# Second down-projection as seven products of quarters, with the quarter sums on GpSimd

## The chip, the cores and the metric

The kernel runs on one core of a Trainium2 chip. The time is device microseconds of one execution: 2637.14 us is the median of three runs before the change (2635.62 to 2639.12).

A core has engines with a queue of their own each: TensorE (PE in the profile; PEld is its loading of weights), VectorE (DVE), ScalarE (ACT), GpSimd (POOL) and SyncE (SP), which issues all DMAs here. Matrix products land in PSUM, eight banks of 128x512 numbers; all other tiles lie in SBUF.

## The reference: what is computed

One layer over 1024 latent tokens (and 256 context tokens) of width 1024: a half-step SwiGLU, two attention mixers with a merge, and a second half-step SwiGLU. The change is in the last of these:

```python
def _swiglu(h, w1, w3, w2):
    return (jax.nn.silu(h @ w1) * (h @ w3)) @ w2
...
        x = _residual(x, _swiglu(_modnorm(x, g[4], m[6], m[7]), ffn2_w1[l], ffn2_w3[l], ffn2_w2[l]),
                      g[5], m[8], HALF_STEP)
```

`D_FF` is 2816, so the last product is [1024 tokens x 2816] times [2816 x 1024]. `_residual` normalises each token's row of the product, scales it by a gate, and adds it to x.

## The kernel before, in words

*Precision.* Every float32 operand of a large product is split in two: `split` (L202) lets ACT cast it to the high part and DVE subtract that from the operand for the low part. `mm3` (L158) then issues three matmuls: high with high, high with low, low with high. A matmul has a 128x128 stationary and a 128x512 moving operand and writes one bank.

*Pools.* SBUF tiles come from pools: `U` and `V` (24 and 16 tiles of 128x1024), `T2` (20 tiles of 128x512). PSUM banks have the tags s, m and v (3, 3 and 2 buffers).

*Order.* The kernel's author writes the order out: a `Plan` (L163) has main steps, most of them groups of matmuls, and `spread` puts side work (loads, splits, sums) behind the main steps with given numbers. Engines keep this order, and each waits for what it needs by semaphores. `store` (L134) issues its DMA some main steps later (2 if no number is given), so that SP is not held.

*Second up-projection* (`up_units`, L700). `Unit` (L494) makes 256 rows of h @ w1 or h @ w3 from quarters, by seven products of 12 matmuls in place of eight; the sums that this takes are made by DVE from SBUF (`Unit.sum`) or while it empties banks (`p6`, `p5`, `p7`, `p3`, `p4`). A w1 unit and a w3 unit make a pair, eleven pairs in all; `emit1` applies SiLU, `emit3` multiplies and stores the gated quarter, 128 rows of D_FF by 512 tokens, into a DRAM tensor. The first 14 units are led: their first two products run ahead as one step each (`plan_leads`), and five are left. The other 8 run whole, seven products. A product of 12 matmuls is one main step.

*Second down-projection* (`Down`, L729). It walks over the 22 chunks of 128 rows of D_FF in ten groups, nine of two chunks and one of four. In each group every one of the 8 token tiles and 2 output halves gets a bank, 3 matmuls per chunk; ACT copies the first group's banks into the output tiles (V), DVE adds those of the others. Gated rows and weights come back from DRAM as 128x1024 tiles and are split, three steps ahead and more. Beside it runs `ada_steps((8,))`: the row of the last modulation, 16 DVE operations of 128x512. `gate_rows` turns it into a row for all tokens (8 small transposes).

*End* (L2066 to L2118). With the last group each finished token tile is squared by ACT, POOL makes the reciprocal root (two operations of 128x1), DVE multiplies by the gate, scales and adds x, and SP stores. The last tile goes in halves.

Of the kernel before, what the change touches and what calls it, by code (L numbers as in the profile page):

```python
# [10 lines left out]
BF16 = mybir.dt.bfloat16  # L11
# [32 lines left out]
def hybrid_block(ctx: ExitStack, tc: tile.TileContext, a: dict, out: bass.AP):  # L44
# [25 lines left out]
    def V(dt=F32):  # L70
        return U(dt, "v")
# [16 lines left out]
    def PB(tag):  # L88
        return ps.tile([P, 512], F32, tag=tag, name=nm("b" + tag), bufs=PBUFS[tag])
# [22 lines left out]
    class Engine:  # L112


        def __init__(self, e):
            self.e = e
# [132 lines left out]
    class Ada:  # L249
# [20 lines left out]

        def turn(self):
            rows = self.rows
            pt = PB("v").rearrange("p (t g c) -> p t g c", t=4, c=32)
# [41 lines left out]
    class AdaSum(Ada):  # L315


        def __init__(self, m):
            self.m = m
            self.acc = [[T2() for _ in range(2)] for _ in range(2 if m < 5 else 1)]  # L320

        def load(self, k, h):
# [10 lines left out]
                    vec.scalar_tensor_tensor(t[h], r, sc[:, k, v:v + 1], t[h], op0=ALU.mult, op1=ALU.add)  # L333

        def add_up(self):
            self.bank = PB("v")
# [9 lines left out]
    def ada_steps(ms):  # L346

        s = []
        cur = {}

        def step(m, k, h):
            if m not in cur:
                cur[m] = AdaSum(m)
# [28 lines left out]
    def gate_rows(col, key="u"):  # L382
        row = U(key=key)
        for h in range(2):
            pb = PB("s")
            for k in range(4):
                turn_(pb[:, k * P:(k + 1) * P], col[:, 4 * h + k:4 * h + k + 1].to_broadcast([P, P]), ident)
            act.copy(row[:, h * 512:(h + 1) * 512], pb)
        return row
# [307 lines left out]
                plan.spread([f], at[t] + x, at[t] + x + 1)  # L697


    def up_units(h, w1, w3, gd):  # L700

        units = []

        def pair_(p):
            s = {}

            def emit1(i, ci, x, bank):
                s[i, ci] = T2() if bank else x
# [12 lines left out]
        return units  # L721
# [7 lines left out]
    class Down:  # L729
# [26 lines left out]
        def tile(self, t, es=range(2)):  # L756
            ys, fs = self.ys, self.fs
            g = self.g if t < 8 else self.c
            c = slice((t % 8) * P, (t % 8 + 1) * P)
            if fs[0] == 0 and 0 in es:  # L760
                ys[t] = V()
            for e in es:
                o = slice(e * 512, (e + 1) * 512)
                pd = PD()
                for x, f in enumerate(fs):
                    mm3(pd, [y[:, c] for y in g[f]], self.w[f][e], x == 0, x == len(fs) - 1)
                if fs[0] == 0:
                    act.copy(ys[t][:, o], pd)
                else:
                    vec.tensor_tensor(ys[t][:, o], ys[t][:, o], pd, op=ALU.add)  # L770

    def groups(sizes):
# [1222 lines left out]
    gd2 = DR([NF, P, NLAT])  # L1995
    units2 = up_units(h3, a["f2w1"], a["f2w3"], gd2)
    plan = Plan()
    for f in set0[6:] + wsets[1].loads():
# [51 lines left out]
    plan.spread([normal_banks], e - 1, e)  # L2050
    plan_rest(plan, units2)

    gs = groups((2,) * 9 + (4,))
    ys2 = {}
    downs2 = [Down(a["f2w2"], gd2, ys2, fs) for fs in gs]
    o = len(plan.main)
    plan.spread([lambda: downs2[0].loads(0, "u")], o - 9, o - 8)
    plan.spread(downs2[0].steps(key="u"), o - 7, o)

    def last_col():  # L2060
        cols["g8"] = gate_col(8, 5, 0, 0.5)

    def last_gates():
        cols["g8"] = gate_rows(cols["g8"], "v")

    def done2(t, x):  # L2066
        y = ys2[t]
        if x == 0:
            xr, r, z = V(), rstd(y, D), V()
# [10 lines left out]
    def done_half(e):  # L2080

        y, o = ys2[7], slice(e * 512, e * 512 + 512)
        if e == 0:
            end.update(x=V(), z=V(), ss=ST(2), junk=T2(BF16, 1024))
            ld(end["x"], x2s[7 * P:8 * P, :])
        z, ss = end["z"], end["ss"]
        act.activation(end["junk"][:, o], y[:, o], AF.Square, scale=D ** -0.5, accum_out=ss[:, e:e + 1])
        if e == 0:
            pool.tensor_scalar(ss[:, 0:1], ss[:, 0:1], EPS, None, op0=ALU.add)
            vec.tensor_tensor(z[:, o], y[:, o], cols["g8"][:, o], op=ALU.mult)  # L2090
            return
        r = ST()
        act.activation(ss[:, 1:2], ss[:, 1:2], AF.Identity, bias=ss[:, 0:1])
        pool.tensor_tensor(r, ss[:, 1:2], mhalf[:, 0:1], op=ALU.pow)
        vec.tensor_tensor(z[:, o], y[:, o], cols["g8"][:, o], op=ALU.mult)
        for h in range(2):
            o = slice(h * 512, h * 512 + 512)
            vec.scalar_tensor_tensor(z[:, o], z[:, o], r, end["x"][:, o], op0=ALU.mult, op1=ALU.add)
            store(out[7 * P:8 * P, o], z[:, o], 0)

    d2_at = len(plan.main)
    for i, d in enumerate(downs2):
        o = len(plan.main)
        if i + 1 < len(downs2):
            plan.step(*[lambda d=d, t=t: d.tile(t) for t in range(8)])
        else:
            plan.step(*[lambda d=d, t=t: d.tile(t) for t in range(7)], *[lambda d=d, e=e: d.tile(7, (e,)) for e in range(2)])
        if i + 1 < len(downs2):
            n = downs2[i + 1]
            plan.spread([lambda n=n: n.loads(n.fs[0])], o - 1, o)  # L2110
            plan.spread(n.steps(), o + 1, o + 8)
        else:
            plan.spread([last_col], o - 3, o - 2)
            plan.spread([last_gates], o - 1, o)
            for t in range(7):
                plan.spread([lambda t=t: done2(t, 0)], o + t, o + t + 1)
                plan.spread([lambda t=t: done2(t, 1)], o + t + 1, o + t + 2)
            plan.spread([lambda e=e: done_half(e) for e in range(2)], o + 7, o + 9)  # L2118
# [80 lines left out]
```

## Time and profile before

| what | value |
|---|---|
| median of the runs | 2637.14 us |
| profiled execution, span of its instructions | 2632.2 us |
| PE busy | 2602.1 us, 13728 matmuls |
| DVE busy | 1854.2 us |
| ACT busy | 1151.8 us |
| POOL busy | 220.3 us, 368 instructions |
| second up-projection, after the leading products | 2041.2 to 2383.7 us |
| second down-projection | 2383.7 to 2625.2 us |
| DMA in all | 414.14 MB, mean 157 GB/s |

The profiled execution's own time is known by its span alone, from its first instruction to its last; the runs' times hold a few microseconds around it. Start times count from the span's start. A row of a timeline has the start, the length, the engine, the line, the operation, the tiles written and read (buffer numbers left out) and, in brackets, the idle time before it and what ended that. A row of groups has the number of instructions, their busy time, the mean length of one in ns, and the idle time before them with its releasers. Tiles are named by pool: xu, xv and t for U, V and T2, bs, bm and bv for the banks, st for small statistics, d for DRAM. The line of most instructions is that of a helper (L120 for DVE, ACT and POOL, L153 for matmuls, L132 for DMAs), so the tiles tell more.

### The profile page before, as it was taken

The numbers are of one execution on the slowest core, as the hardware profiler recorded it, in microseconds if no ns is written. First come the engines' busy times: TensorE is split into PE (matmuls) and PEld (weight loads), VectorE is DVE, ScalarE is ACT, GpSimd is POOL, SyncE is SP. The second block draws the span as 40 slices with busy tenths as digits, with TensorE's granted clock in tenths as the row PEclk, the third lists the DMA queues.
The fourth block names the chain that finished last, engine by engine and source line by source line (L and its number), as shares of the span: only waits on it lengthen the run. The fifth ranks groups of instructions, "written<-read, shape, count | busy, mean of one in ns | idle before, by whom it ended". The sixth has DMA issues, their size and how long they took to land.

```text
span 2632.2 us, 37730 instructions
## 1 busy us (share of the span) xinstructions
PE 2602.1 (99%) x13728; PEld 2215.3 (84%) x13728; DVE 1854.2 (70%) x3478; ACT 1151.8 (44%) x2193; POOL 220.3 (8%) x368
## 2 busy tenths in 40 slices
PE   8999999999999999999999999999999999999998
PEld 6888888888888788889889999987888888888887
DVE  4778876588776676864569988877436777565876
ACT  6622223522223753433439887772365222234111
POOL 1000000000000400001004422220020000000001
PEclk9999999999999999999999999999999999999999
DMA  8544433444433665745977723217244433225333
GB/s 303 166 157 145 150 106 125 157 160 161 163 130 99 229 227 188 247 150 181 304 285 281 211 75 75 67 49 230 86 148 166 138 120 109 76 92 193 120 96 128
DMA packets 196218, 414.14 MB, mean 157 GB/s; under 512 B 24960, under 2 KB 66112, under 8 KB 196032
## 3 DMA queue, kind: packets, MB, share of 16 engines
q1 hardware_dynamic: 196032, 411.73, 47.3%
q8 instruction: 108, 1.77, 0.3%
q14 instruction: 78, 0.64, 0.1%
HBM read 308.30 MB, written 103.35 MB: 156 GB/s over the span
## 4 chain that ended last, share of the span: by engine, by line
PE 56%; issue 32%; DVE 5%; ACT 5%; DMA 1%; POOL 1%; SPq 0%; DVEq 0%; POOLq 0%; ACTq 0%
PE bs L153 23%; PE bm L153 17%; PE bv L153 13%; PE bm L156 2%; ACT xu L1775 1%; DVE xu L1639 1%; DVE t L1802 1%; ACT t L1801 1%; DVE xv L120 1%; PE bs L156 1%; POOL st L120 1%; ACT t L120 1%; DVE t L120 1%; DVE xu L120 1%; ACT t L1775 0%
## 5 line engine op out<-in xcount | busy, mean ns | idle before, releaser
L153 PE MATMUL bm<-xu,xu 128*128 128x512 f32 (+2 forms) x2376 | 569.4, 388 | 0.9 <-ACT t L120 0.6
L153 PEld LDWEIGHTS bm<-xu,xu 128*128 128x128 f32 x2376 | 437.5, 188 | 89.9 <-ACT t L120 1.9
L153 PE MATMUL bs<-xu,xu 128*128 128x512 f32 (+1 forms) x1800 | 433.5, 385 | 0.0
L153 PEld LDWEIGHTS bs<-xu,xu 128*128 128x128 f32 x1800 | 332.3, 188 | 67.4 <-issue 0.8
L153 PE MATMUL bs<-xv,xu 128*128 128x512 f32 x1488 | 357.3, 389 | 0.3 <-DVE t L120 0.3
L153 PE MATMUL bv<-xv,xu 128*128 128x512 f32 x1342 | 335.4, 389 | 0.0
L153 PEld LDWEIGHTS bs<-xv,xu 128*128 128x128 f32 x1488 | 279.2, 188 | 58.6 <-issue 0.7
L120 ACT CAST xu<-t 128x512 fp32r<-128x512 f32 x260 | 158.2, 616 | 355.8 <-DVE t L120 354.6
L153 PEld LDWEIGHTS bv<-xv,xu 128*128 128x128 f32 x1342 | 251.9, 188 | 52.3
L120 DVE TENSOR_TENSOR xu<-t,xu 128x512 fp32r<-128x512 f32 x260 | 178.5, 688 | 127.2 <-ACT xu L120 127.2
L120 DVE TENSOR_TENSOR xu<-xv,xu 128x512 fp32r<-128x512 f32 (+2 forms) x244 | 182.3, 767 | 57.1 <-ACT xu L120 54.0
L153 PE MATMUL bs<-w,w 96*128 96x512 f32 (+3 forms) x832 | 206.2, 366 | 2.5 <-DVE st L1664 2.2
L120 POOL TENSOR_SCALAR st<-st 128x1 f32<-128x1 f32 (+1 forms) x66 | 34.6, 524 | 1977.8 <-ACT t L120 1959.4
L120 DVE TENSOR_TENSOR xu<-xu,xu 128x512 fp32r<-128x512 f32 (+1 forms) x218 | 151.0, 698 | 67.1 <-ACT xu L120 66.7
L120 ACT CAST xu<-xv 128x512 fp32r<-128x512 f32 (+2 forms) x216 | 136.8, 692 | 125.9 <-DVE xv L120 60.3
L153 PE MATMUL bm<-t,xu 128*128 128x256 f32 (+1 forms) x1272 | 165.3, 287 | 0.6 <-ACT t L120 0.4
L153 PEld LDWEIGHTS bm<-t,xu 128*128 128x128 f32 x1272 | 160.7, 191 | 6.0 <-ACT t L120 0.8
L153 PE MATMUL bv<-xu,xu 128*128 128x512 f32 x602 | 161.7, 389 | 0.0
L120 ACT ACTIVATE t<-t 128x512 f32<-128x512 f32 (+1 forms) x94 | 57.3, 609 | 221.6 <-DVE t L120 212.6
L153 PE MATMUL bv<-t,w 128*128 128x256 f32 x896 | 151.5, 288 | 2.7 <-DVE t L1802 2.0
L153 PEld LDWEIGHTS bv<-t,w 128*128 128x128 f32 x896 | 132.8, 189 | 18.5 <-DVE t L1802 6.8
L120 ACT CAST xu<-xu 128x512 fp32r<-128x512 f32 (+1 forms) x218 | 134.2, 627 | 15.8 <-DMA xu<-in_f1w 8.1
(216 smaller groups left out, 3679.2 us busy)
## 6 DMA issues: line engine op xcount, KB each, us to landing
d<-t SPq DMA_DIRECT2D x272, 256.0 KB, 2.8
xv<-d SPq DMA_DIRECT2D x68, 512.0 KB, 4.5
xv<-in_f1w SPq DMA_DIRECT2D x64, 512.0 KB, 3.6
xu<-in_f1w SPq DMA_DIRECT2D x61, 512.0 KB, 3.8
xu<-in_f2w SPq DMA_DIRECT2D x60, 512.0 KB, 3.8
t<-in_wada SPq DMA_DIRECT2D x112, 256.0 KB, 3.9
t<-d SPq DMA_DIRECT2D x76, 256.0 KB, 3.3
xu<-in_winT SPq DMA_DIRECT2D x38, 512.0 KB, 4.6
```

The lines of the kernel that those rows point to most:

```text
L120: return lambda *x, **y: pin(f(*x, **y))
L153: return pin(nc.tensor.matmul(o, s, m, start=start, stop=stop, skip_group_check=open_group[0]))
L156: return pin(nc.tensor.transpose(o, x, i))
L1639: nc.vector.tensor_scalar(dst, src, 1.0, FMIN, op0=ALU.mult, op1=ALU.max, accum_out=m)
L1775: nc.scalar.activation(x, x, AF.Exp, bias=n_[:, s:s + 1], accum_out=l[:, i:i + 1])
L1801: nc.scalar.copy(t[0], pb)
L1802: nc.vector.tensor_tensor(t[1], pb, f32(t[0]), op=ALU.subtract)
```

## The change

The down-projection is done like the units: with A the gated rows (tokens in halves, D_FF in halves by pairs of chunks) and B the weights, in quarters, seven products replace eight. Three of A's four quarters and four sums of them, s1 to s4, enter as left operands; B's quarters and t1 to t4 as right ones.

- In the up-projection, `Gated.put` stores three quarters of each pair, keeps all four in SBUF, and after the last one lets GpSimd make s1 = a21 + a22, s3 = a11 - a21, s2 = s1 - a11 and s4 = a12 - s2, which are stored too, four steps later. For led pairs a11 was made long before and is loaded back.
- The down stage (`Quarters`) has 77 steps: 7 products, each over 11 pairs, 12 matmuls a step, 3 for each of four token tiles, in four banks that stay open over the 11 steps. Products 1 and 2 share banks, as do 3 and 4, and 5, 6 and 7. At the end of each product the four banks are copied (1 and 2, ACT) or added with an output tile's half (DVE) to where they belong. The last four steps go by token tile in place of by pair, so that the tiles finish one after the other.
- Each step's operands are loaded seven steps ahead and split three steps ahead, into V tiles. W2's quarters stay in 22 U tiles; GpSimd makes t1 = b12 - b11, t3 = b22 - b12, t2 = b22 - t1 and t4 = b21 - t2 in their place. Planned steps: t1 at 9 to 19, t3 and t2 at 26 to 36, t4 at 37 to 47.
- The modulation row is spread over steps 12 to 38 with its bank from tag s; tiles 0 to 3 are finished during product 6, tiles 4 to 7 in halves, the upper half first.

There are 132 matmuls fewer and 88 GpSimd operations more, and SP issues 1384 DMAs in place of 1264.

```diff
+    class Gated:
+        def __init__(self):
+            self.d = {(n, p): DR([P, 512]) for n in ("a11", "a12", "a22", "s1", "s2", "s3", "s4") for p in range(NP)}
+            self.t = {}
+        def put(self, p, i, ci, y, again):
+            name = f"a{ci + 1}{i + 1}"
+            if name != "a21":
+                store(self.d[name, p], y)
+            if name != "a11" or not again:
+                self.t[name] = y
+            if name == "a22" and again:
+                t = self.t["a11"] = T2()
+                ld(t, self.d["a11", p])
+            if name == "a21":
+                self.sums(p)
+        def sums(self, p):
+            a11, a12, a21, a22 = [self.t.pop(n) for n in ("a11", "a12", "a21", "a22")]
+            s1, s4 = T2(), T2()
+            pool.tensor_tensor(s1, a21, a22, op=ALU.add)
+            pool.tensor_tensor(a21, a11, a21, op=ALU.subtract)
+            pool.tensor_tensor(a11, s1, a11, op=ALU.subtract)
+            pool.tensor_tensor(s4, a12, a11, op=ALU.subtract)
+            for n, x in (("s1", s1), ("s3", a21), ("s2", a11), ("s4", s4)):
+                store(self.d[n, p], x, 4)
...
                 vec.tensor_tensor(y, x, y, op=ALU.mult)
-                store(gd[2 * p + i, :, ci * 512:(ci + 1) * 512], y)
+                if isinstance(gd, Gated):
+                    gd.put(p, i, ci, y, units[2 * p + 1].led)
...
+    class Quarters:
+        ORDER = (("a11", "b11"), ("a12", "b21"), ("s1", "t1"), ("s4", "b22"), ("s2", "t2"), ("s3", "t3"), ("a22", "t4"))
+        BANKS = (("s", "s", "s", "m"), ("m", "m", "v", "v"))
+        LAST = 4
...
+        def split(self, n, key="v"):
+            a = split(self.ra.pop(n), key=key)
+            self.sp[n] = a, split(self.slot(self.ORDER[n // NP][1], n % NP), key=key)
+        def sum(self, name, p):
+            out, x, y = {"t1": ("t1", "b12", "b11"), "t3": ("t3", "b22", "b12"),
+                         "t2": ("t2", "b22", "t1"), "t4": ("t4", "b21", "t2")}[name]
+            pool.tensor_tensor(self.slot(out, p), self.slot(x, p), self.slot(y, p), op=ALU.subtract)
...
+        def product(self, n, j):
+            a, b = self.sp[n]
+            q, p = divmod(n, NP)
+            open_group[0] = True
+            mm3(self.pb[j], [x[:, j * P:(j + 1) * P] for x in a], b, p == 0 and q in (0, 2, 4), p == NP - 1)
+            open_group[0] = False
+        def step(self, n):
+            if n in (0, 2 * NP, 4 * NP):
+                self.banks(n == 2 * NP)
+            if n < self.n - self.LAST:
+                for j in range(4):
+                    self.product(n, j)
+                self.sp.pop(n)
+                if n % NP == NP - 1:
+                    for j in range(4):
+                        self.out(n // NP, j)
+            else:
+                j = n - self.n + self.LAST
+                for x in range(self.n - self.LAST, self.n):
+                    self.product(x, j)
+                self.out(6, j)
...
+        def plan(self, plan, ahead=3, loads=4):
+            o = len(plan.main)
+            at = lambda n: o + n
+            for n in range(self.n):
+                plan.spread([lambda n=n: self.load_a(n)], at(n) - ahead - loads, at(n) - ahead - loads + 1)
+                x = min(at(n) - ahead, at(self.n - self.LAST) - 1)
+                plan.spread([lambda n=n: self.split(n)], x, x + 1)
+                plan.step(lambda n=n: self.step(n))
+            for p in range(NP):
+                for name, first in (("b11", 0), ("b21", NP), ("b12", 6), ("b22", NP + 10)):
+                    x = at(first + p) - ahead - loads
+                    plan.spread([lambda name=name, p=p: self.load_b(name, p)], x, x + 1)
+                for name, x in (("t1", NP - 2 + p), ("t3", 2 * NP + 4 + p), ("t2", 2 * NP + 4 + p), ("t4", 3 * NP + 4 + p)):
+                    plan.spread([lambda name=name, p=p: self.sum(name, p)], at(x), at(x) + 1)
...
-    downs2 = [Down(a["f2w2"], gd2, ys2, fs) for fs in gs]
+    down2 = Quarters(a["f2w2"], gd2, ys2)
...
-    plan.spread(ada_steps((8,)), d2_at + 8, len(plan.main) - 20)
+    plan.spread(ada_steps((8,), "s"), d2_at + 12, d2_at + 38)
```

More of the change, by code (lines that the diff above doesn't have):

```diff
@@ L272, in turn @@
             rows = self.rows
-            pt = PB("v").rearrange("p (t g c) -> p t g c", t=4, c=32)
+            pt = PB(self.tag).rearrange("p (t g c) -> p t g c", t=4, c=32)
             for t in range(2):
@@ L315, in hybrid_block, with __init__ @@
     class AdaSum(Ada):
-        def __init__(self, m):
-            self.m = m
+        def __init__(self, m, tag="v"):
+            self.m, self.tag = m, tag
             self.acc = [[T2() for _ in range(2)] for _ in range(2 if m < 5 else 1)]
@@ L335, in add_up @@
         def add_up(self):
-            self.bank = PB("v")
+            self.bank = PB(self.tag)
             for v, t in enumerate(self.acc):
@@ L344, in hybrid_block, with ada_steps @@
     cols = {}
-    def ada_steps(ms):
+    def ada_steps(ms, tag="v"):
         s = []
@@ L352, in step @@
             if m not in cur:
-                cur[m] = AdaSum(m)
+                cur[m] = AdaSum(m, tag)
             if k:
@@ L713, in emit3 @@
                 vec.tensor_tensor(y, x, y, op=ALU.mult)
-                store(gd[2 * p + i, :, ci * 512:(ci + 1) * 512], y)
+                if isinstance(gd, Gated):
+                    gd.put(p, i, ci, y, units[2 * p + 1].led)
+                else:
+                    store(gd[2 * p + i, :, ci * 512:(ci + 1) * 512], y)
             for w, emit in ((w1, emit1), (w3, emit3)):
@@ L1994, in hybrid_block @@
     ready = {0: [], 1: []}
-    gd2 = DR([NF, P, NLAT])
+    gd2 = Gated()
     units2 = up_units(h3, a["f2w1"], a["f2w3"], gd2)
@@ L2051, in hybrid_block @@
     plan_rest(plan, units2)
-    gs = groups((2,) * 9 + (4,))
     ys2 = {}
-    downs2 = [Down(a["f2w2"], gd2, ys2, fs) for fs in gs]
-    o = len(plan.main)
-    plan.spread([lambda: downs2[0].loads(0, "u")], o - 9, o - 8)
-    plan.spread(downs2[0].steps(key="u"), o - 7, o)
+    down2 = Quarters(a["f2w2"], gd2, ys2)
     def last_col():
@@ L2063, in last_gates @@
     def last_gates():
-        cols["g8"] = gate_rows(cols["g8"], "v")
+        cols["g8"] = gate_rows(cols["g8"])
     def done2(t, x):
@@ L2068, in done2 @@
         if x == 0:
-            xr, r, z = V(), rstd(y, D), V()
+            xr, r, z = U(), rstd(y, D), U()
             ld(xr, x2s[t * P:(t + 1) * P, :])
@@ L2078, in hybrid_block, with done_half @@
     end = {}
[L2080 to L2094, printed above, removed]
+    def done_half(t, e):
+        y, o = ys2[t], slice(e * 512, e * 512 + 512)
+        if e == 1:
+            end[t] = dict(x=U(), z=U(), ss=ST(2))
+            ld(end[t]["x"], x2s[t * P:(t + 1) * P, :])
+        z, ss = end[t]["z"], end[t]["ss"]
+        junk = T2(BF16, 1024)
+        act.activation(junk[:, 0:512], y[:, o], AF.Square, scale=D ** -0.5, accum_out=ss[:, e:e + 1])
+        if e == 1:
+            pool.tensor_scalar(ss[:, 1:2], ss[:, 1:2], EPS, None, op0=ALU.add)
+        else:
+            act.activation(ss[:, 0:1], ss[:, 0:1], AF.Identity, bias=ss[:, 1:2])
+            r = end[t]["r"] = ST()
+            pool.tensor_tensor(r, ss[:, 0:1], mhalf[:, 0:1], op=ALU.pow)
@@ L2095, in done_half, with done_end @@
         vec.tensor_tensor(z[:, o], y[:, o], cols["g8"][:, o], op=ALU.mult)
+    def done_end(t):
+        x, z, r = [end[t][n] for n in "xzr"]
         for h in range(2):
             o = slice(h * 512, h * 512 + 512)
[L2098 to L2118, printed above, removed]
@@ L2119, in hybrid_block @@
-    plan.spread(ada_steps((8,)), d2_at + 8, len(plan.main) - 20)
+            vec.scalar_tensor_tensor(z[:, o], z[:, o], r, x[:, o], op0=ALU.mult, op1=ALU.add)
+            store(out[t * P:(t + 1) * P, o], z[:, o], 0)
+    d2_at = down2.plan(plan)
+    e = len(plan.main)
+    plan.spread(ada_steps((8,), "s"), d2_at + 12, d2_at + 38)
+    plan.spread([last_col], d2_at + 39, d2_at + 40)
+    plan.spread([last_gates], d2_at + 40, d2_at + 41)
+    for j in range(4):
+        o = d2_at + 5 * NP + 2 * j
+        plan.spread([lambda j=j: done2(j, 0)], o, o + 1)
+        plan.spread([lambda j=j: done2(j, 1)], o + 1, o + 2)
+        o = e - 9 + j
+        plan.spread([lambda j=j: done_half(4 + j, 1)], o, o + 1)
+        o = e - 4 + j
+        plan.spread([lambda j=j: done_half(4 + j, 0)], o, o + 1)
+        if j:
+            plan.spread([lambda j=j: done_end(3 + j)], o, o + 1)
@@ L2120, in hybrid_block @@
+    plan.spread([lambda: done_end(7)], e - 1, e)
     plan.run()
```

35 lines of the change are left out of this document (added).

## The prediction

> **What bounds the kernel now.** I read the page first (span, engines, clock), then the stretches of the three stages that the change touches, then the chain that ended last, and at last single stretches of time on DVE and GpSimd (POOL).
>
> ```profile
> span 2632.2 us, 37730 instructions
> PE 2602.1 (99%) x13728; PEld 2215.3 (84%) x13728; DVE 1854.2 (70%) x3478; ACT 1151.8 (44%) x2193; POOL 220.3 (8%) x368
> ```
> ```profile
> 2041.20:2231.60 190.40, 190.40 (x841) 157.66 (x841) 137.07 (x216) 53.40 (x91) 0.00 (x0) 1.00 0.38 122
> 2231.60:2383.70 152.10, 152.10 (x672) 125.94 (x672) 93.83 (x146) 47.23 (x83) 0.00 (x0) 1.00 0.26 87
> 2383.70:2625.20 241.50, 241.50 (x1075) 199.10 (x1073) 170.83 (x241) 61.02 (x94) 11.30 (x15) 1.00 0.40 134
> ```
> ```profile
> 2139.10 2.72 PE bv L153 x12
> ```
> ```profile
> 2398.70 1.52 PE L153 MATMUL bm<-xu,xu 128*128 128x512 f32 x6
> 2400.05 1.52 PE L153 MATMUL bv<-xu,xu 128*128 128x512 f32 x6
> ```
>
> The columns of the stretches are length, then busy time of PE, PEld, DVE, ACT and POOL, granted clock, DMA share and GB/s. The rows are the second up-projection with led units, with whole units, and the second down-projection. PE is never idle in them and runs at full clock, so PE's matmuls are the time, and POOL is free but for 11.30 us at the end. The chain row gives the price: 12 matmuls in 2.72 us, 0.2267 us each. Six to a bank start 1.35 us apart (2398.70 to 2400.05), the same price, so how often PE changes bank costs nothing that shows.
>
> **Removed from PE.** Before: 22 rows of chunks x 8 tiles x 2 halves x 3 = 1056 matmuls, 239.4 us. After: 7 products x 11 pairs x 4 tiles x 3 = 924 in 77 steps of 12, 209.4 us. The gate's transposes and the sums of the modulation row are the same 18 small ones. Saved: 132 x 0.2267 = 29.9 us, all of it on the path.
>
> **DVE and ACT in the down stage.** A step needs two splits, each one ACT cast and one DVE subtraction; the 144 additions into the output tiles fall to 20, and copies from 16 to 8.
>
> ```profile
> L120 DVE TENSOR_TENSOR xu<-xv,xu 128x512 fp32r<-128x512 f32 x40 | 27.3, 686 | 10.3 <-ACT xu L120 10.3
> L120 ACT CAST xu<-xv 128x512 fp32r<-128x512 f32 x40 | 23.7, 619 | 106.8 <-DVE xv L120 60.3 <-PE bm L153 46.0
> L120 DVE SCALAR_TENSOR_TENSOR t<-t,sc,t 128x512 f32<-128x512 f32 x14 | 10.4, 746 | 0.0
> ```
>
> ACT: 2 x 0.62 = 1.24 of 2.72 us, hidden. DVE: 2 x 0.69, and one row of the modulation sums (0.75) in steps 12 to 30: 2.1 of 2.72 us at most, hidden as long as nothing else holds DVE.
>
> **The GpSimd sums: their length.** 88 are added, 128x512 with two inputs from SBUF; no such row exists. The nearest:
>
> ```profile
> L1617 POOL TENSOR_TENSOR t<-t,t 64x256 f32<-64x256 f32 x32 | 23.5, 734 | 102.3 <-DVE t L1616 84.1 <-DVE st L1671 13.5 <-PE bs L153 4.7
> L1619 POOL CAST xo<-t 64x256 fp32r<-64x256 f32 x64 | 25.6, 400 | 4.1
> L1631 POOL COPY rope<-st 128x256 f32<-128x256 f32 x32 | 12.7, 398 | 168.3 <-DVE st L1677 150.9 <-DVE st L1779 17.0
> 2589.11 0.19 POOL L120 TENSOR_SCALAR st<-st 128x1 f32<-128x1 f32 x1 [621.20 <-ACT t L120]
> ```
>
> 128 partitions cost what 64 do (0.398 and 0.400). With one element at 0.19 us, 512 elements take 0.19 + 2 x (0.734 - 0.19) = 1.28 us; bounds: 1.09 without the fixed part, 1.47 as twice the row.
>
> **What a sum does to DVE.** Here the saving can go.
>
> ```profile
> 1509.35 0.73 POOL L1617 TENSOR_TENSOR t<-t,t 64x256 f32<-64x256 f32 x1 [5.63 <-DVE t L1616]
> 1509.58 0.52 DVE L1778 TENSOR_TENSOR st<-st 128x2 f32<-128x2 f32 x1
> L1778 DVE TENSOR_TENSOR st<-st 128x2 f32<-128x2 f32 x32 | 5.3, 164 | 0.3 <-ACT t L1775 0.3
> 2594.40 1.22 DVE L120 TENSOR_TENSOR xv<-xv,xv 128x1024 f32<-128x1024 f32 x1
> 2594.55 1.11 POOL L120 TENSOR_SCALAR st<-st 128x1 f32<-128x1 f32 x1 [4.62 <-DVE xv L120]
> ```
> ```profile
> 1510.09 0.67 DVE L1699 TENSOR_TENSOR t<-bm,t 128x512 fp32r<-128x512 f32 x1
> 1510.14 0.40 POOL L1619 CAST xo<-t 64x256 fp32r<-64x256 f32 x1
> ```
>
> A DVE operation of 0.16 us with both inputs in SBUF that starts inside a POOL sum takes 0.52 and ends at 1510.10, with the sum (1510.08). The other way round a POOL operation of 0.19 takes 1.11 and ends at 2595.66, with DVE's (2595.62). So the two exclude each other and take turns. DVE ended 0.02 after POOL though it needs 0.16 itself: POOL's last 0.14 us do not hold it. I therefore take 1.09 us of hold for each sum; ends 0 (no hold, against these rows) and 1.47. An operation with one input from PSUM (1510.09) and a POOL cast beside it keep their 0.67 and 0.40 us, so I count the additions from PSUM as free of it. A subtraction in a row of its kind takes 0.60 (below: 2180.54 to 2181.14), so sum and subtraction in turn take 1.69 us.
>
> [...] What the whole 1.28 would give is the second rival.
>
> **Sums of the gated rows, up-projection.** Four sums follow each other after a pair's last gated quarter. Its stretch before the change:
>
> ```profile
> 2178.41 0.69 DVE L120 TENSOR_TENSOR t<-t,t 128x512 f32<-128x512 f32 x1
> 2179.02 0.68 DVE L120 TENSOR_TENSOR xu<-t,xu 128x512 fp32r<-128x512 f32 x1
> 2180.54 0.68 DVE L120 TENSOR_TENSOR t<-xu,t 128x512 f32<-128x512 f32 x1
> 2181.14 0.69 DVE L120 TENSOR_TENSOR xu<-xu,xu 128x512 fp32r<-128x512 f32 x1
> 2183.26 0.68 DVE L120 TENSOR_TENSOR xu<-t,xu 128x512 fp32r<-128x512 f32 x1
> 2183.86 0.68 DVE L120 TENSOR_TENSOR t<-xu,xu 128x512 f32<-128x512 f32 x1
> 2185.38 0.69 DVE L120 TENSOR_TENSOR t<-t,bs 128x512 f32<-128x512 f32 x1 [0.83 <-PE bs L153]
> 2187.43 0.69 DVE L120 TENSOR_TENSOR xu<-t,xu 128x512 fp32r<-128x512 f32 x1 [0.76 <-ACT xu L120]
> 2190.61 2.88 PE L153 MATMUL bs<-xv,xu 128*128 128x512 f32 x12
> ```
>
> The quarter is ready at 2179.10. In turns, with 1.09: the split of 2179.02 to 2179.62, sum one to 2180.71, quarter sum (was 2180.54) to 2181.31, sum two to 2182.40, split to 2183.00, sum three to 2184.09, split (was 2183.26) to 2184.69, sum four to 2185.78, then 2183.86's to 2186.4. The addition of 2185.38 is 1.0 late; PE needs its bank 2.72 after the product it reads. The split of 2187.43 ends about 1.0 late, at 2189.1, and PE needs it at 2190.61: no stall. Four times 0.38 more (hold 1.47) still just fits. In whole units DVE is 94/152 busy against 137/190, so there is more room. Price 0. The four stores of the sums come to SP four steps, 10.9 us, behind the quarter; the sums end 6.7 us behind it, so the weight loads queued after them don't wait. 33 more quarter stores, 7 loads back, and in all 120 more DMA issues stand against a DMA share of 0.26 to 0.40: free.
>
> **Start of the down stage.** The last pair's four sums and eleven t1 sums (each needs only its W2 quarters loaded and its first one split) are all but ready at once. Splits 0 and 1 are done, so seven sums are waiting. While they wait each step's two splits take 2 x 1.69 = 3.38 us, and the queue falls by one per step: splits 2 to 8 take 23.7, from 1.6 us after the last product (0.2 for the wait and two operations of 0.69). Split 8 is there at 25.3; PE wants it at 8 x 2.72 = 21.8: 3.5 us lost (8.8 with 1.47). After that a step holds one sum and two subtractions, 2.29 us: no loss.
>
> **Middle of the down stage.** t2 overwrites t1, so it waits for t1's split; t3 and t2 alternate in POOL's queue, t4 stand behind them (wanted by the splits of product 7 alone, from step 63 on, so their own lateness costs nothing). From the end of step 21 on, splits 24 to 37 (28 subtractions, 7 modulation rows) meet 28 sums that are always ready: nine t2, eight t3, eleven t4. Turns: 28 x 1.09 + 35 x 0.60 = 51.5 us. PE has two steps in hand (ACT's copies of step 21 stand before split 24) and needs 13 steps more: 15 x 2.72 = 40.8. Lost: 10.7 us (21.4 with 1.47). The additions after step 32 read PSUM, and two sums pass beside them. From split 38 on nothing contends, and the splits run ahead again.
>
> **Edges.** Products 2, 4, 6 and 7 write on into the banks of the one before, behind four copies or additions. Each bank has 9 matmuls, 2.0 us, between its last write and the next, against 0.7 us: free where DVE is not late, and counted above where it is. The tail is as before, addition, square, power, two halves, store: 7.0 us from the end of the last row of PE, 2625.2.
>
> ```profile
> 2622.32 2.88 PE L153 MATMUL bs<-xu,xu 128*128 128x512 f32 x12
> ```
>
>
> **Sum.** -29.9 + 0 + 3.5 + 10.7 = -15.7 us on the profiled 2632.2: 2616.5. The median of the runs, 2637.1, is 4.9 above that span (work around it), so 2621.4.
>
> **Rivals.**
> - *No hold*: subtractions pass beside the sums. For it: the pair at 1510 that passes beside; against it the pairs at 1509 and 2594. All 29.9 stay: 2607.2. Chance 0.10.
> - *Whole instruction*: hold 1.28. Start 1.6 + 7 x 3.76 - 21.8 = 6.1, middle 28 x 1.28 + 21.0 - 40.8 = 16.0: 2637.1 - 7.8 = 2629.3. Chance 0.22.
> - *Slower*: a sum of 128x512 holds DVE far longer than twice the small one. At a hold of H the down stage loses 14.2 + 42 x (H - 1.09); this eats the saving at 1.46, and above 1.47 the seven led pairs stall too, four times the excess each. At 1.8: 44.0 + 7 x 1.3 = 53.1, so +23: 2660. For it: no sum of this size is in the trace; against it the 0.734 mean of 32 small ones, which leaves little but the elements to grow. Chance 0.22.
> - *Forecast* (hold 1.0 to 1.2): 2617 to 2626. Chance 0.46.
>
> [...]
>
> **How the numbers follow.** 0.2% (5.3 us) is about what the runs can tell from no change. Faster: 0.46 + 0.10 + 0.13 of the second rival = 0.69; same: 0.09 of it and 0.02 of the slower one; slower 0.20. The range goes from no hold, 2606, to a little over hold 1.47, 2643.
>
> **What would show it.** PE at 13596 matmuls; 88 POOL sums of 128x512, unblocked near 1.28; PE idle, released by DVE's subtractions into the split tiles, near steps 6 to 10 and 26 to 37 and nowhere else, 14 us in all; those subtractions far over 0.69 on average there. It is wrong if PE idles in the up-projection, if it idles without DVE standing beside a sum, or if a sum takes over 1.5 us.

## The result, and the profile after

The changed kernel takes 2625.31 us, the median of five runs (2623.75 to 2627.11), against 2636.24 us (2633.22 to 2639.12) for the kernel before in the same comparison. The ratio is 0.9958, 95% interval 0.9946 to 0.9971: faster by 0.42%, 10.9 us. The forecast was 2621.4 us with a range of 2606 to 2643, so the time lies inside the range, 3.9 us above the forecast. The profiled span fell from 2632.2 to 2622.0 us, 5.5 us above the 2616.5 forecast for it. Each run of the changed kernel is about 1.8 us longer than its own span (2623.75 for 2622.0, 2627.11 for 2625.3).

The head of the profile's page, first the span, then busy time, share and instruction count of each engine:

```profile
span 2622.0 us, 38011 instructions
PE 2577.2 (98%) x13596; PEld 2191.1 (84%) x13596; DVE 1891.3 (72%) x3448; ACT 1190.2 (45%) x2282; POOL 371.9 (14%) x456
```

PE has the 13596 matmuls that were counted, 132 fewer. By stretches (length, busy time of PE, PEld, DVE, ACT and POOL, granted clock, DMA share, GB/s), the last part of the up-projection and then the down stage in four pieces:

```profile
2231.00:2383.40 152.40, 152.40 (x674) 126.21 (x674) 104.64 (x145) 51.42 (x92) 24.59 (x16) 1.00 0.36 120
2383.40:2410.00 26.60, 25.69 (x111) 20.29 (x110) 26.46 (x21) 6.86 (x12) 22.66 (x14) 1.00 1.01 358
2410.00:2503.00 93.00, 80.08 (x342) 63.27 (x341) 80.80 (x80) 34.74 (x62) 57.02 (x35) 0.96 0.57 194
2503.00:2556.00 53.00, 53.00 (x241) 43.93 (x240) 29.32 (x49) 23.63 (x42) 0.00 (x0) 1.00 0.14 44
2556.00:2622.00 66.00, 57.95 (x255) 47.38 (x253) 47.94 (x70) 30.34 (x64) 20.28 (x16) 0.96 0.48 172
```

The up-projection is as before: PE busy in all of it, ending at 2383.36 instead of 2383.74. What is new is PE standing still in the down stage: 0.9 us in the second row, 12.9 in the third, and 1.0 in the last beside the tail, with the granted clock at 0.96 in the third row (in the last row the lower clock lies behind PE's last matmul). These are PE's stalls, from the timeline of PE; the bracket at the end is the idle time ahead of the row and what ended it (steps of 12 matmuls, 2.72 us each when nothing stalls):

```profile
2397.53 2.14 PE L153 MATMUL bs<-xv,xv 128*128 128x512 f32 x8 [0.18 <-DVE xv L120]
2404.33 2.11 PE L153 MATMUL bs<-xv,xv 128*128 128x512 f32 x8 [0.39 <-DVE xv L120]
2409.68 2.20 PE L153 MATMUL bs<-xv,xv 128*128 128x512 f32 x9
2459.91 1.42 PE L153 MATMUL bm<-xv,xv 128*128 128x512 f32 x5 [0.89 <-DVE xv L120]
2480.16 1.43 PE L153 MATMUL bm<-xv,xv 128*128 128x512 f32 x5 [1.01 <-DVE xv L120]
2481.43 1.52 PE L153 MATMUL bv<-xv,xv 128*128 128x512 f32 x6
2489.84 2.90 PE L153 MATMUL bm<-xv,xv 128*128 128x512 f32 x6 [6.89 <-DVE xv L120]
2494.61 1.55 PE L153 MATMUL bm<-xv,xv 128*128 128x512 f32 x6
2584.76 2.29 PE L153 MATMUL bs<-xv,xv 128*128 128x512 f32 x9 [0.98 <-DVE xv L120]
```

Step k would start at 2383.36 + k x 2.72. Step 9 starts at 2409.68 instead of 2407.84: the start of the stage costs 1.84 us, in steps 5 to 7 (first two rows). Steps 27 to 32 stall once each (the fourth and fifth rows are the first and the last of six). Step 33 could start 1.36 after 2481.43, at 2482.79, instead of 2474.96 with the 1.84 carried along, so these six cost 7.83. Step 33 starts at 2489.84: 7.05 more. Its matmuls are slow (granted clock 0.50 from 2487.18 to 2494.01), and step 34 starts 4.77 behind it: 2.05 more. Step 66 waits 0.98 and starts 1.14 late. The sum is 19.9 us, of which PE stands idle for 14.8; the rest is slow matmuls and about 0.3 us more than the idle time at each of the smaller stalls. From the end of the up-projection to the end the stage took 248.5 us before and 238.6 after, 9.8 less, and 29.9 - 19.9 is 10.0.

**Turns.** GpSimd and VectorE at the start of the stage and in the middle of it (timeline of the changed kernel):

```profile
2385.11 6.72 POOL L120 TENSOR_TENSOR t<-t,t 128x512 f32<-128x512 f32 x4 [30.64 <-DVE t L120]
2391.79 11.93 POOL L120 TENSOR_TENSOR xu<-xu 128x512 f32<-128x512 f32 x7
...
2437.73 2.54 POOL L120 TENSOR_TENSOR xu<-xu,xu 128x512 f32<-128x512 f32 x2 [0.62 <-DVE xv L120]
...
2459.93 3.42 POOL L120 TENSOR_TENSOR xu<-xu,xu 128x512 f32<-128x512 f32 x2 [0.63 <-DVE xv L120]
```
```profile
2385.50 1.78 DVE L120 TENSOR_TENSOR xv<-xu,xv 128x512 fp32r<-128x512 f32 x1
2387.20 1.77 DVE L120 TENSOR_TENSOR xv<-t,xv 128x512 fp32r<-128x512 f32 x1
...
2404.20 0.68 DVE L120 TENSOR_TENSOR xv<-t,xv 128x512 fp32r<-128x512 f32 x1
...
2459.78 0.74 DVE L120 SCALAR_TENSOR_TENSOR t<-t,sc,t 128x512 f32<-128x512 f32 x1
2460.44 1.78 DVE L120 TENSOR_TENSOR xv<-t,xv 128x512 fp32r<-128x512 f32 x1
2462.14 1.77 DVE L120 TENSOR_TENSOR xv<-xu,xv 128x512 fp32r<-128x512 f32 x1
```

A subtraction that meets a sum takes 1.77 us and follows the one before by 1.70: its own 0.60 in a row, and 1.09 to 1.10 more for the sum. This extra time of VectorE is what is called the hold. Where nothing stands against it (2437.73, two sums that VectorE is idle beside) a sum takes 1.27 us. Both are close to the forecast, 1.09 and 1.28. In the middle each step has a row of the modulation and two subtractions that meet two sums, 0.66 + 2 x 1.70 = 4.06 us (4.05 from 2459.78 to the next such row, at 2463.83) where PE needs 2.72; that is the 1.33 by which each of the steps 28 to 32 is late.

### The profile page after: what moved, and what is told of

Read it like the earlier page. It is cut to its first block, busy times and chain, and to the rows that moved or that the text cites. A ratio compares the mean times of both kernels' runs of the same rounds, so it can differ in the third digit from the quotient of the medians.

```text
span 2622.0 us, 38011 instructions
## 1 busy us (share of the span) xinstructions
PE 2577.2 (98%) x13596; PEld 2191.1 (84%) x13596; DVE 1891.3 (72%) x3448; ACT 1190.2 (45%) x2282; POOL 371.9 (14%) x456
## 3 DMA queue, kind: packets, MB, share of 16 engines
q8 instruction: 107, 1.75, 0.3%
## 5 line engine op out<-in xcount | busy, mean ns | idle before, releaser
L153 PE MATMUL bm<-xu,xu 128*128 128x512 f32 (+1 forms) x1980 | 469.6, 388 | 0.6 <-DVE xu L120 0.3
L153 PEld LDWEIGHTS bm<-xu,xu 128*128 128x128 f32 x1980 | 363.4, 188 | 73.9 <-ACT t L120 1.4
L153 PE MATMUL bs<-xu,xu 128*128 128x512 f32 (+1 forms) x1404 | 334.0, 384 | 0.0
L153 PEld LDWEIGHTS bs<-xu,xu 128*128 128x128 f32 x1404 | 258.0, 188 | 52.0 <-issue 0.8
L120 POOL TENSOR_SCALAR st<-st 128x1 f32<-128x1 f32 (+1 forms) x66 | 42.6, 646 | 1413.2 <-ACT t L120 1402.8
L120 DVE TENSOR_TENSOR xu<-xu,xu 128x512 fp32r<-128x512 f32 (+1 forms) x212 | 161.3, 766 | 65.9 <-ACT xu L120 65.5
L120 DVE TENSOR_TENSOR xu<-xv,xu 128x512 fp32r<-128x512 f32 (+4 forms) x196 | 141.4, 744 | 42.0 <-ACT xu L120 38.8
L120 ACT CAST xu<-xu 128x512 fp32r<-128x512 f32 (+1 forms) x212 | 130.2, 624 | 14.9 <-DMA xu<-in_f1w 7.8
L153 PEld LDWEIGHTS bs<-w,w 96*128 96x128 f32 (+1 forms) x832 | 123.6, 190 | 10.8 <-DVE st L1798 3.5
L1936 DVE TENSOR_TENSOR t<-bm,t 128x512 fp32r<-128x512 f32 x160 | 110.0, 688 | 27.7 <-ACT t L1935 27.2
```

Source lines behind the costliest of these rows:

```text
L120: return lambda *x, **y: pin(f(*x, **y))
L153: return pin(nc.tensor.matmul(o, s, m, start=start, stop=stop, skip_group_check=open_group[0]))
L1936: nc.vector.tensor_tensor(t[1], pb, f32(t[0]), op=ALU.subtract)
```

## The experiments

The part ahead of the down stage has the same code in all these kernels, but moved by some us from profile to profile (the last pair's four sums start at 2385.11 in the changed kernel and at 2389.30 in the latest). What moved it was not shown. So stages are compared by their length from the first of those four sums to the end of the span: 236.9 us in the changed kernel. Without any stall it would be 216.8 (248.5 - 29.9 less the 1.75 from the last up-projection matmul to that sum).

Theory: a GpSimd sum with both inputs in SBUF takes 1.09 us from VectorE, whoever needs the result; PE loses what VectorE then lacks. Rivals: the waits for the sums' results; the order of VectorE's queue at the ends of products; VectorE's amount of work.

### t4 later

```
-                    "b21": (1, 0), "t4": (1, 0), "b22": (1, 1)}[name]
+                    "b21": (1, 0), "t4": (0, 0), "b22": (1, 1)}[name]
```

> Edit: t4 is written over t2 instead of over b21, so it waits for t2's split (steps 41 to 51); all else as in the changed kernel (profiled span 2622.0, stalls 1.9 at the start, 8.0 in steps 27 to 32, 7.1 before step 33, 2.0 of low clock behind that, 1.0 at step 66). Theory of turns (each GpSimd sum with both inputs in SBUF takes 1.09 us from VectorE): the 8.0 stay, since only t2 and t3 run in those steps; before step 33 VectorE has two rows of the modulation, one split and the additions at their own 0.6 to 0.7 us, so the stall falls from 6.9 to about 2.9, and the slow matmuls behind it go; the t4 sums meet one split per step later, 1.20 + 1.09 = 2.3 of 2.72 us, and cost nothing. Span about 2616. Rival (the stall before step 33 comes from the wait of the product for its bank's additions, whatever GpSimd does): 2622, stall 6.9 still there.

The t4 sums did not move: in the order of the program they still stood ahead of t2's splits, so they had nothing to wait for. (The fifth product then reads t4 in t2's place, so this kernel computes something else.) The time was 2626.3 us (ratio 0.9962, 0.9947 to 0.9977), and the longest stall is the same 6.8 us. The row of PE's waits (total, count, longest):

```profile
PE bm L153 <- DVE xv L120: 12.9, 7, 6.8
```

It decides nothing. The next kernel also moves them in the queue:

```
-  for name, x in (..., ("t4", 3 * NP + 4 + p)):
+  for name, x in (..., ("t4", 4 * NP + 4 + p)):
```

> Edit: t4 is written over t2 and stands eleven places later in GpSimd's queue, so it waits for t2's split (steps 41 to 51); t1, t2 and t3 as in the changed kernel. Theory of turns: the 8.0 us of steps 27 to 32 stay (t2 and t3 alone run there); before step 33 VectorE has two rows of the modulation, one split and the first addition at 0.6 to 0.7 us, so the stall falls from 6.9 to about 2.9 us, and the low clock behind it gets shorter or goes; the t4 sums meet one split per step later, 1.20 + 1.09 = 2.3 of 2.72 us, and cost nothing. Span 2616 to 2618. Rival (the stall before step 33 is the wait for the additions, whatever GpSimd does): 2622.

```profile
2486.93 0.74 DVE L120 SCALAR_TENSOR_TENSOR t<-t,sc,t 128x512 f32<-128x512 f32 x1
2487.60 1.27 DVE L120 TENSOR_TENSOR xv<-xv,bm 128x512 f32<-128x512 f32 x2
2488.42 1.62 PE L153 MATMUL bm<-xv,xv 128*128 128x512 f32 x6 [2.71 <-DVE xv L120]
2583.07 4.18 PE L153 MATMUL bs<-xv,xv 128*128 128x512 f32 x9 [2.69 <-DVE xv L120]
```

Ahead of step 33 the stall is 2.71 us (2.9 by the theory, 6.9 by the rival), VectorE's row of the modulation takes 0.74, and the matmuls behind it run at full speed; steps 27 to 32 stall as before. So the t4 sums, which nobody needed yet, cost 4 us there; by the rows above, the rest is the additions' place in the queue. The time is not told apart from the changed kernel: 2624.6 us (0.9955, 0.9938 to 0.9971). Of the 6 us won at step 33, step 66 took back most: it waits 2.69 now, and its nine matmuls take 4.18 us instead of 2.29. The stage is 235.4 us, 1.5 shorter. The span of 2616 to 2618 was wrong for that reason (2623.2, which also holds 2.7 us by which the part ahead was longer). That the moved sums cost nothing was wrong too: the last three now run at 2553.97 to 2561.08, ahead of step 66, and the three subtractions that meet them take 1.77 to 1.78 us. That this made the stall at step 66 longer is likely, but no run changes it alone.

### One sum per step

t4 is written over t2, t3 over b22, and the order in GpSimd's queue is t2, t3, t4:

```
-  for name, x in (..., ("t3", 2 * NP + 4 + p), ("t2", 2 * NP + 4 + p), ("t4", 3 * NP + 4 + p)):
+  for name, x in (..., ("t2", 2 * NP + 4 + p), ("t3", 3 * NP + 4 + p), ("t4", 4 * NP + 4 + p)):
```

> Edit: t4 over t2, t3 over b22, and the order in GpSimd's queue t2, then t3, then t4, so that each sum waits for the split of the quarter it overwrites and one sum at most is ready per step. Theory of turns: one sum, two subtractions and (to step 38) one row of the modulation take 1.09 + 1.20 + 0.66 = 2.95 of 2.72 us, so VectorE loses 0.2 to 0.3 per step for 18 steps, 4 to 5 us against two steps (5.4 us) that PE has in hand: the 17 us of the middle fall to 0 to 4. Span 2605 to 2609. Rival (the stalls come from the splits' lead of two steps at the ends of products, not from how many sums are ready): the stall before step 33 stays at 5 us or more, span above 2612.

```profile
2478.74 2.90 PE L153 MATMUL bm<-xv,xv 128*128 128x512 f32 x6 [2.94 <-DVE xv L120]
2575.42 2.30 PE L153 MATMUL bs<-xv,xv 128*128 128x512 f32 x9 [3.36 <-DVE xv L120]
```

2616.7 us, ratio 0.9929 (0.9912 to 0.9946), span 2612.6, stage 226.8: ten us less than the changed kernel with the same sums on the same engine. The stalls in steps 27 to 32 are gone, that ahead of step 33 is 2.94. The forecast of 2605 to 2609 missed by step 66 (3.36, taken as 1.0; three sums meet the splits ahead of it here too) and by the slow matmuls behind 2478.74. The rival's 5 us or more ahead of step 33 are not there, and of 20.1 us lost in the stage 10.0 are left; the span alone, at the rival's bound of 2612, would not have told the two apart.

### The additions first

```
-  x = min(at(n) - ahead, ...)
+  x = min(at(n) - ahead + (n == 3 * NP + 1), ...)
```

> Edit: one line of the plan: the two splits of step 34 are issued one step later, behind the additions of the third product instead of ahead of them. Theory of turns: VectorE's queue is short by what the 28 sums take from it, whatever the order: the stall before step 33 gets shorter by the split's 3.4 us, but the split itself then comes later and stalls step 34 by about as much; at most 1.9 us and the 2.0 us of low clock are won: span 2618 to 2621. Rival (order: PE waits only because the additions stand behind the split and the rows of the modulation): 3.4 us of the stall and the low clock go and do not come back: span 2616 or less.

```profile
2488.47 2.18 PE L153 MATMUL bm<-xv,xv 128*128 128x512 f32 x6 [3.51 <-DVE xv L120]
2502.99 0.44 PE L156 MATMUL bs<-ident,t 128*128 128x128 f32 x2 [0.92 <-DVE t L120]
```

The stall ahead of step 33 is halved, from 6.89 to 3.51, as either theory has it; 0.92 us of it comes back at 2502.99 and 0.5 at step 66 (1.47). The stage is 234.9 us, 2.0 shorter; the time is 2624.0 us (0.9954, 0.9939 to 0.9969), not told apart from the changed kernel. Neither forecast is met in full: step 34, which the theory saw stall, starts without a wait at 2492.89, and the low clock, which both saw go, is still there (0.50 from 2489.5 to 2492.5; step 33 takes 4.42 us instead of 2.72). So the run does not decide between them; it shows that this order is worth about 2 us, a tenth of the loss.

### No quarter sums

The line that does t1 to t4 is left out. (Four products, not five, then read a quarter in place of a sum, so this kernel computes something else.)

> Edit: the 44 sums of the weight quarters (t1 to t4) are left out, so that five of the seven products use unsummed quarters; the sums of the gated rows stay. Theory of turns: the stalls of the start (but for the last pair's four sums, 4.4 us against a lead of two steps: 0) and of the middle go, with the low clock; only the 1.0 us at step 66 is left. Span 2632.2 - 29.9 + 1.0 = 2603.3. Rival (part of the loss is the plan itself: splits three steps ahead, sixteen wide tiles, additions between products): stalls stay in steps 24 to 37, span over 2606.

```profile
2568.47 2.32 PE L153 MATMUL bs<-xv,xv 128*128 128x512 f32 x9 [1.44 <-DVE xv L120]
```

This is the only stall left in the stage. 2606.5 us (0.9887, 0.9872 to 0.9902), span 2605.7, stage 218.5. The span is 2.4 over its forecast, 2.1 of it in the part ahead. The plan of splits, banks and additions costs only this stall: those of the start and the middle are the sums' alone. Whether by their holds or by the waits for their results, this run does not tell.

### The sums on VectorE

```
-  pool.tensor_tensor(self.slot(out, p), self.slot(x, p), self.slot(y, p), op=ALU.subtract)
+  vec.tensor_tensor(self.slot(out, p), self.slot(x, p), self.slot(y, p), op=ALU.subtract)
```

> Edit: the 44 sums of the weight quarters are done by VectorE instead of GpSimd, at the same places of the plan. Theory of turns: a sum costs VectorE its own 0.60 us in a row instead of the 1.09 us for which GpSimd's holds it, and comes when the plan says instead of as soon as it can: four operations and a row of the modulation in steps 26 to 36 are 3.06 of 2.72 us, 3.7 us in all against two steps in hand; the stall of the start goes. Left are 0 to 3 us in the middle and 1.0 to 1.4 at step 66: span 2603 to 2607. Rival (VectorE's own amount of work is the bound, not GpSimd's holds): 44 more operations, 26 us, make it slower than the changed kernel, 2625 or more.

```profile
2464.17 1.28 DVE L120 TENSOR_TENSOR xu<-xu,xu 128x512 f32<-128x512 f32 x2
2475.41 1.60 PE L153 MATMUL bm<-xv,xv 128*128 128x512 f32 x6 [0.25 <-DVE xv L120]
```

2607.7 us, ratio 0.9892 (0.9877 to 0.9907), span 2605.6: one word takes another 17.7 us off. Two sums take VectorE 1.28 us, 1.20 in a row, where two of GpSimd's take 2.18 from it. The stall ahead of step 33 is 0.25. VectorE's amount of work is not the bound.

> Edit: as the run before it, and t3 and t4 at steps 39 and 44 on, one after another, instead of 26 and 37 on: in no step more than 2.7 us for VectorE. Theory of turns: no stall in the start and the middle; 1.0 to 1.4 us at step 66 are left: span 2603 to 2605.

That run also moves t3 and t4:

```
-  for name, x in (..., ("t3", 2 * NP + 4 + p), ("t2", 2 * NP + 4 + p), ("t4", 3 * NP + 4 + p)):
+  for name, x in (..., ("t2", 2 * NP + 4 + p), ("t3", 3 * NP + 6 + p), ("t4", 4 * NP + p)):
```

2607.4 us (0.9892, 0.9877 to 0.9907): no stall but that of step 66, which is 1.96 us instead of the 1.0 to 1.4 forecast; the span, 2606.6, is over its forecast. The time is that of the run before it.

### The residual tiles earlier

Step 66 in the changed kernel: SP's queue and VectorE (timelines).

```profile
2574.23 0.34 SPq L132 DMA_DIRECT2D out_x<-xu  x1
...
2575.28 0.59 SPq L132 DMA_DIRECT2D xu<-d  x1
```
```profile
2580.32 1.29 DVE L120 SCALAR_TENSOR_TENSOR xu<-xu,st,xu 128x1024 f32<-128x1024 f32 x1 [2.58 <-DMA xu<-d]
...
2583.93 1.88 DVE L120 TENSOR_TENSOR xv<-xv,bs 128x512 f32<-128x512 f32 x3
```

In the plan, the load of a residual tile goes out only behind the store of the row before it (2574.23, 2575.28); VectorE's last operation on the row stands 2.58 us at the head of its queue until it lands, with two steps' splits and the additions of the sixth product behind it. The edit, on top of the run before:

```
...
+        if x < 0:
+            cols[t] = U(), U()
+            ld(cols[t][0], x2s[t * P:(t + 1) * P, :])
+        elif x == 0:
+            (xr, z), r = cols[t], rstd(y, D)
...
+        plan.spread([lambda j=j: done2(j, -1)], o - 3, o - 2)
```

> Edit: as the run before it, and the four residual tiles of the first output rows are loaded three steps earlier (their tiles are taken then), so that VectorE's last operation on a row doesn't wait for the load that SP can issue only behind the store of the row before. Theory: the stall at step 66, where the additions of the sixth product stand behind such a wait, goes too: 1.0 to 1.4 us less than the run before it, span 2602 to 2604, and the ratio to the kernel before 0.988 to 0.989. Rival (step 66 waits for its splits or for the loads of the gated sums): the stall stays.

```profile
2389.00:2569.00 180.00, 180.00 (x805) 148.54 (x804) 142.59 (x221) 82.57 (x148) 17.98 (x12) 1.00 0.57 203
```

PE is busy in the whole stage at full clock, up to its last matmul at 2597. Span 2604.3, 0.3 over the forecast, and stage 216.8, which is the length worked out for no stall at all. The time is 2606.2 us, ratio 0.9886 (0.9871 to 0.9901): faster than the kernel before and the changed kernel, but not told apart by the time alone from the two runs before it; the stage is 219.1 in the last of them.

### Sums that nobody waits for

On top of the last kernel, 22 sums on a tile that nothing else reads (the forecast takes 1.70 us a turn):

```
+        x = U()[:, 0:512]
+        pool.memset(x, 0.0)
+        for _ in range(22):
+            pool.tensor_tensor(x, x, x, op=ALU.subtract)
```

> Edit: the best kernel so far (quarter sums by VectorE, spread, residual tiles loaded early: span 2604.3, no stall in the down stage), and 22 sums of 128x512 by GpSimd on a tile of its own that nothing else reads, issued at the first step of the down stage behind the last pair's four gated sums. Theory of turns: 26 GpSimd sums meet 26 of VectorE's operations, each turn 1.70 us, to about 44 us behind the first; VectorE then has split 13 just ready where PE wants it at 13 x 2.72 = 35.4, so PE loses 8 to 9 us and the subtractions of these steps show 1.77 us: span 2612 to 2614. Rival (it was the wait for the results of the sums that cost the time, and the long subtractions are only how waits are recorded): nothing waits for these, span 2604 to 2605.

```profile
2394.17 31.88 POOL L120 TENSOR_TENSOR xu<-xu 128x512 f32<-128x512 f32 x22
```
```profile
2394.70 1.52 DVE L120 TENSOR_TENSOR xv<-t,xv 128x512 fp32r<-128x512 f32 x1
2396.14 1.53 DVE L120 TENSOR_TENSOR xv<-xu,xv 128x512 fp32r<-128x512 f32 x1
```
```profile
2422.31 2.14 PE L153 MATMUL bs<-xv,xv 128*128 128x512 f32 x8 [1.31 <-DVE xv L120]
```

Nobody waits for these sums, VectorE's subtractions are held all the same, and PE stalls where the theory puts it, in steps 13 and 14, by 1.3 us each. The time is 2610.7 us (0.9907, 0.9891 to 0.9924), an interval that overlaps that of the last kernel; the evidence is in the rows and in the stage of 220.2, 3.4 us longer than without these sums. It is not 8 to 9 longer, and the span of 2607.1 is under the forecast: with one tile for both inputs and the output the turn is 1.45 us, a hold of 0.85. 22 times 0.24 less is 5.3 us, which is the miss.

The next kernel has one input, `pool.tensor_scalar(x, x, 0.0, None, op0=ALU.add)`, in their place:

> Edit: as the run before it, with 22 GpSimd operations of one input (a constant added) on the same tile in place of the sums. Worked out from 0.40 us for a cast of 256 columns and 0.19 for one element: about 0.6 us each unblocked. If one input from SBUF is enough to hold VectorE's operations with two: turns of about 0.6 + 0.4 to 0.6 us, subtractions of 1.1 to 1.3 us in place of 0.69 for some 22 operations, but 2 x 1.2 = 2.4 of 2.72 us a step, so PE loses nothing: span 2604 to 2605. If one input doesn't hold: the same span, the subtractions at 0.69 us.

```profile
2397.10 1.09 DVE L120 TENSOR_TENSOR xv<-t,xv 128x512 fp32r<-128x512 f32 x1
2398.12 0.68 DVE L120 TENSOR_TENSOR xv<-xu,xv 128x512 fp32r<-128x512 f32 x1
```
```profile
2411.55 7.80 POOL L120 TENSOR_SCALAR xu<-xu 128x512 f32<-128x512 f32 x5
```

Every second subtraction takes 1.09, 0.41 more than its 0.68, so one input from SBUF was enough to hold VectorE. These operations are not the 0.6 us long that was worked out: five of them beside an idle VectorE take 7.80 us, 1.56 each. So an operation that is longer than a sum (1.27) holds VectorE for less (0.41 against 1.09). PE loses nothing: stage 216.8, 2607.6 us (0.9896, 0.9881 to 0.9910).

## Why the prediction was right, and where it was not

**Removed from PE, 29.9.** Right: 13596 matmuls, and the kernel without a stall has the stage at 216.8 us.

**Up-projection, 0.** Right: no stall of PE in it, though the sums take 1.59 us there on average, blocked time included. By the letter, the sign that a sum over 1.5 us would refute the forecast came true, but it was badly put: 1.27 is a sum without VectorE beside it, 1.6 to 1.7 one that waits for its turn.

**Hold of 1.09 us, turns of 1.69.** Right: 1.67 to 1.71 from row to row. "No hold" would have given 2607.2, which is about what the kernels without GpSimd's quarter sums reach; "whole instruction" needed a hold of 1.28. The hold measured is shorter than the operation that causes it: 1.09 of 1.27 us, and with one input 0.41 of 1.56.

**Start of the down stage, 3.5.** Over-sized: 1.84. Fourteen turns were counted in a row (splits 2 to 8), the rows show eleven sums in a row (four and seven, 2385.11 to 2403.72); from 2404.20 on only one subtraction of a split meets a sum.

**Middle of the down stage, 10.7.** The mechanism was right and the term too small: 14.9 us of stalls (7.83 and 7.05) and 2.05 of slow matmuls. One step of it was wrong by count, "PE has two steps in hand":

```profile
2447.59 0.74 DVE L120 SCALAR_TENSOR_TENSOR t<-t,sc,t 128x512 f32<-128x512 f32 x1
2447.76 1.52 PE L153 MATMUL bm<-xv,xv 128*128 128x512 f32 x6
```

When the turns begin, at 2447.6, PE is only starting step 23: one step in hand, and 14 x 2.72 = 38.1 in place of 40.8. With 51.5 us of turns that is 13.4. The other failing step was under Edges, "free where DVE is not late, and counted above where it is": it was late, and the count did not hold it. The four additions that step 33 needs stand behind split 34 and two rows of the modulation:

```profile
2482.33 1.77 DVE L120 SCALAR_TENSOR_TENSOR t<-t,sc,t 128x512 f32<-128x512 f32 x1
2484.02 1.74 DVE L120 TENSOR_TENSOR xv<-t,xv 128x512 fp32r<-128x512 f32 x1
...
2487.35 1.74 DVE L120 SCALAR_TENSOR_TENSOR t<-t,sc,t 128x512 f32<-128x512 f32 x1
2489.02 1.27 DVE L120 TENSOR_TENSOR xv<-xv,bm 128x512 f32<-128x512 f32 x2
```

So PE waits with the split of step 33 done (at 2482.40) and cannot use it. Between 13.4 and 14.9 lie 1.5 us; the run with the additions first won 2.0 of stage, which fits, though part of that is the low clock.

**Low clock and step 66.** Neither stood in the sum: 2.05 and 1.14 us. "Nowhere else" was wrong for step 66, where VectorE waits for a load and no sum is beside it. That is one of the prediction's own signs of being wrong, and it holds for these 1.1 of the 19.9 us.

**Work around the span, 4.9.** Wrong: each run is about 1.8 us longer than its own span, in the later runs of the kernel before too (2635.94 for 2634.1). The other 3.1 were the distance of one profiled execution from a median. The changed kernel's profiled execution lies only 1.6 below its median, so 1.6 us of the miss do not show in the time: 3.9 instead of 5.5. That is luck, and so is that the start's term was too large where the middle's was too small. PE's idle time, 14.8 us, is near the 14 of the forecast, but the loss is 19.9.

By terms: -29.9 + 1.8 + 14.9 + 2.0 + 1.1 = -10.1 against the forecast's -15.7 and the span's -10.2.

## What to carry to other kernels

An elementwise sum that moved from VectorE to an idle GpSimd was not free for VectorE here: it cost 1.09 us of it, and doing the sum itself 0.60. GpSimd ran its queue as soon as data were there, not where the plan has them (the t1 sums, planned behind step 9, which starts at 2409.68, began at 2391.79), so sums that are wanted later must be held back by what they overwrite, and the queue's order must agree. Where products end, look at what stands in VectorE's queue ahead of the additions that free the banks; a lead in splits did not help PE past them here (step 33 has its split at 2482.40 and starts at 2489.84).

## What the runs showed of the hardware that was not expected

The granted clock can fall to one half after PE stands still, and stay there though PE works again. The changed kernel around the stall of 6.89 us (the columns as above):

```profile
2483.00:2487.00 4.00, 0.00 (x0) 0.00 (x0) 4.00 (x3) 1.12 (x2) 4.00 (x4) 1.00 0.31 78
2487.00:2488.00 1.00, 0.00 (x0) 0.00 (x0) 1.00 (x2) 0.00 (x0) 1.00 (x1) 0.59 0.58 211
2488.00:2490.00 2.00, 0.16 (x1) 0.19 (x2) 2.00 (x3) 0.00 (x0) 2.00 (x2) 0.50 0.00 0
2490.00:2494.00 4.00, 4.00 (x10) 3.13 (x11) 4.00 (x6) 0.00 (x0) 4.00 (x4) 0.50 0.42 119
2494.00:2495.00 1.00, 1.00 (x6) 0.82 (x5) 1.00 (x1) 0.19 (x1) 1.00 (x2) 1.00 0.13 47
```

The run with t4 later, at step 33 and at step 66, and the run with one sum per step, at the same two:

```profile
2485.00:2488.40 3.40, 0.71 (x4) 0.25 (x3) 3.40 (x7) 1.14 (x2) 0.00 (x0) 1.00 0.52 175
2488.40:2491.00 2.60, 2.58 (x11) 2.16 (x12) 2.60 (x5) 0.00 (x0) 0.00 (x0) 1.00 0.40 132
2580.00:2583.00 3.00, 0.38 (x2) 0.00 (x0) 3.00 (x6) 0.37 (x1) 0.00 (x0) 0.91 0.70 228
2583.00:2586.00 3.00, 2.93 (x7) 2.38 (x8) 3.00 (x6) 1.98 (x4) 0.00 (x0) 0.50 1.00 351
```
```profile
2475.50:2478.50 3.00, 0.30 (x2) 0.00 (x0) 3.00 (x4) 1.14 (x2) 1.68 (x2) 0.95 0.54 143
2478.50:2481.50 3.00, 2.76 (x7) 2.21 (x8) 3.00 (x6) 0.00 (x0) 0.63 (x1) 0.50 0.35 122
2572.00:2575.40 3.40, 0.05 (x1) 0.01 (x1) 3.40 (x7) 0.72 (x2) 0.00 (x0) 1.00 0.63 213
2575.40:2578.00 2.60, 2.58 (x11) 2.16 (x12) 2.60 (x5) 1.85 (x4) 0.00 (x0) 1.00 1.02 336
```

In the changed kernel the clock falls at 2487.18, 4.2 us after PE stopped, and comes back at 2494.01, 4.2 us after it works again: ten matmuls in the 4.00 us from 2490.00. The length of the stall doesn't decide alone: 2.69 us ahead of step 66 brought a clock of 0.50 and slow matmuls in the run with t4 later (9 in 4.18 us), 2.94 ahead of step 33 with one sum per step (6 in 2.90), but 2.71 ahead of step 33 and 3.36 ahead of step 66, in the same two kernels, did not (clock 1.00, 6 in 1.62, 9 in 2.30). What tells these apart was not shown.
